# Chunk products of a gated linear recurrence: from 128-token tiles to pairs of 64-token tiles in the matmul array

## The chip, the cores and the metric

The kernel runs on one core of a Trainium2 chip. The metric is the device time of one execution, in microseconds; lower is better. Three executions of the kernel before took 3016.31, 3017.25 and 3018.32 us, median 3017.25 us. The inputs are float32. Matrix products are made by TensorE (PE in the profile) from an SBUF operand that is loaded into the array first (`lhsT`, the weights) and one that is streamed past it (`rhs`, the moving operand), into PSUM. VectorE (DVE), ScalarE (ACT) and GpSimd (POOL) do the rest, and most transfers are issued from SyncE's queue (SP).

## The reference

One decoder layer for 2048 prompt tokens and 32 sample tokens: norm and input projection, then a gated linear recurrence (HGRN2, 4 heads of 128 features) beside a dilated window attention, output projection, a gated feed-forward block with a short convolution, and a gated embedding. The change touches the recurrence of the prompt alone. Cut to that:

```python
def gla_chunked(q, k, v, logf, s0, chunk):
    """S_t = diag(f_t) S_{t-1} + k_t v_t^T, o_t = S_t^T q_t, evaluated chunkwise."""
    ...
    def step(s, xs):
        qc, kc, vc, gc = xs
        b = jnp.cumsum(gc, axis=2)
        o_inter = jnp.einsum('bhtk,bhkv->bhtv', qc * jnp.exp(b), s)
        diff = b[:, :, :, None, :] - b[:, :, None, :, :]
        decay = jnp.exp(jnp.where(causal[:, :, None], diff, -jnp.inf))
        scores = jnp.einsum('bhtk,bhsk,bhtsk->bhts', qc, kc, decay)
        o = o_inter + jnp.einsum('bhts,bhsv->bhtv', scores, vc)
        b_last = b[:, :, -1]
        s = jnp.exp(b_last)[..., None] * s + jnp.einsum(
            'bhsk,bhsv->bhkv', kc * jnp.exp(b_last[:, :, None] - b), vc)
        return s, o
```

with k = 1 - f. The decay between two tokens s < t is a product of the f of the tokens between them, separately for each feature, so `scores` is no plain matrix product.

## The kernel before, in words

The program has four stages that follow each other on PE. First the input projection of prompt tokens 0 to 1023 (block 0, to about 315 us of the profile's span). Then the input projection of the other 1024 prompt tokens and the 32 sample tokens (block 1, `in_phase(1, ...)`, about 315 to 835 us). Then the attention (about 835 to 1235 us), and the rest of the layer (`trunk`). The projections are made with a hi/lo split of both operands, three matmuls for one (lines 142 to 144 and 344 to 346), accumulated over eight k tiles.

The recurrence works in units: `hgrn_unit` does 512 tokens of two heads. There are 8 units (4 stretches of tokens, 2 pairs of heads). It is a generator that yields between its steps; `first(side, n)` advances it by n steps after each step of the main work, with a higher priority in the scheduler. Units 0 to 6 run inside block 1, and unit 7 (`apart=True`, with more yields) runs inside the attention. A scheduler then sets the order on each engine by its own estimates; only in the attention is PE's order that of the code. Every engine works its own list in order.

In a unit, tokens are the columns and the 128 features the partitions. Per head it loads `q`, `f`, `g` (128 x 512, pieces of 2 KB) and `v` (line 446, pieces of 512 bytes), and makes `F` = 1 - f (the keys, line 448) and `E` = q f (line 450). The 512 tokens are four chunks of 128. A chunk's scores (source token s by target token t, tile `at`) are gathered in parts:

- The diagonal s = t: `F` times `q`, one matmul of 128 x 128 per chunk (line 460), then a product with the identity on DVE that also clears the rest of `at` (line 461).
- Three levels, `LEVELS` = 1, 4, 16. A level with width hw handles the pairs of blocks of hw tokens and of 2 hw tokens: it collects the columns of `E` that belong to right-hand blocks in tile `M` (named `hM`), three groups of 64 columns per chunk (two copies on ACT, lines 469 and 474, one product on POOL, line 476). It multiplies `F` of the chunk with these 192 columns (`level_products`, line 484, four matmuls per head and level), grows `E` and `F` by the decays of the level on DVE (`scale`, line 423, and `grow`), and writes the parts of the result that belong to this level into `at` by six masked copies of 128 x 128 (`copy_predicated`, line 496).
- The last level, 64 by 64 tokens of a chunk, has a matmul of its own with 64 columns of weights (line 516) and a copy into the upper right quarter of `at` (line 520).

Then `F` is transposed (529), the state is advanced (541, 545), the output is `at` times `v` plus `E` times the state (552, 553), normed, transposed (574) and written out (576). `E` of the next unit goes into a buffer that is free once line 553 of the unit before has read it.

Matmuls on float32 operands stand in the trace as two records each, with a weight load each: line 484 has 336 matmul records in units 0 to 6, for 168 matmuls. A matmul with 64 columns of weights has the shape 128*64 in the profile, and with `tile_position=(0, 64 * half)` it sits in one half of the array's columns. Line 822 (attention) already does that, with the halves taking turns. Line 338 does it with quarters (128*32).

The quoted code is that of before:

Of the kernel before, what the change touches and what calls it, by code (L numbers as in the profile page):

```python
# [20 lines left out]
D = 1024  # L21
# [26 lines left out]
def hymba_step_kernel(ctx: ExitStack, tc: tile.TileContext, I: dict, O: dict):  # L48
# [386 lines left out]

    def hgrn_unit(u, heads, S, ld, wk, sp, plv, po, pms, msk, apart=False):

        u0 = 512 * u
        st = {}
        for h in heads:  # L440
            t = {}
            for nm, src in (("f", ha_d[1]), ("q", ha_d[0]), ("g", ha_d[2])):
                t[nm] = ld.tile([128, 512], F32, name="h" + nm)
                SP.dma_start(t[nm], src[:, h, u0:u0 + 512])
            t["v"] = ld.tile([128, 4, 128], F32, name="hv")
            SP.dma_start(t["v"], va_d[u0:u0 + 512, 128 * h:128 * h + 128].rearrange("(c s) d -> s c d", s=128))
            t["F"] = wk.tile([128, 512], F32, name="hF")
            G.tensor_scalar(t["F"], t["f"], -1.0, 1.0, op0=ALU.mult, op1=ALU.add)
            t["E"] = wk.tile([128, 512], F32, name="hE")
            G.tensor_mul(t["E"], t["q"], t["f"])  # L450
            t["D"] = t["f"]
            t["at"] = wk.tile([128, 4, 128], F32, name="at", bufs=4)
            st[h] = t
        yield
        for h in heads:
            t = st[h]
            ps = plv([128, 4, 128])
            for c in range(4):
                cs = slice(128 * c, 128 * c + 128)
                PE.matmul(ps[:, c], lhsT=t["F"][:, cs], rhs=t["q"][:, cs], start=True, stop=True)  # L460
            V.tensor_mul(t["at"], ps, ident.rearrange("p (o t) -> p o t", o=1).to_broadcast([128, 4, 128]))
        yield

        def level_operands(t, hw):
            E, D = t["E"], t["D"]
            M = t["M"] = wk.tile([128, 3, 4, 64], F32, name="hM")
            slots = lambda i, n: M[:, i].rearrange("p c (n h) -> p (c n) h", h=n)
            er = pairs(E, hw)[1]
            A.copy(slots(0, hw), er)
# [4 lines left out]
            A.copy(slots(1, 2 * hw), er)  # L474
            d = D.rearrange("p (n four) -> p n four", four=4)[:, :, 1:2]
            G.tensor_mul(slots(2, 2 * hw), er, d.to_broadcast(list(er.shape)))

        def level_products(t):
            pss = t["pss"] = []
            for i in range(2):  # L480
                ps = plv([128, 512])[:, :384].rearrange("p (a c t) -> p a c t", a=3, c=2)
                for c in range(2):
                    cc = 2 * i + c
                    PE.matmul(ps[:, :, c], lhsT=t["F"][:, 128 * cc:128 * cc + 128], rhs=t["M"][:, :, cc],  # L484
                              start=True, stop=True)
                pss.append(ps)

        def level_results(t, li, hw):
# [3 lines left out]
            t["D"] = D4  # L492
            for j in range(2):
                at = t["at"][:, 2 * j:2 * j + 2].rearrange("p c t -> p (c t)")
                for a, n in enumerate((hw, 2 * hw, 2 * hw)):
                    V.copy_predicated(pairs(at, n)[1], msk[:, 3 * li + a].rearrange("p (n h) -> p n h", h=n),
                                      t["pss"][j][:, a].rearrange("p c (n h) -> p (c n) h", h=n))

        for li, hw in enumerate(LEVELS):
            for h in heads:  # L500
                level_operands(st[h], hw)
                if not apart:
                    level_products(st[h])
            for h in heads:
                if apart:
                    yield
                    level_products(st[h])
                    yield
                level_results(st[h], li, hw)
            yield  # L510
        for h in heads:
            t = st[h]
            E, F = t["E"], t["F"]
            ps = plv([128, 4, 128])
            for c in range(4):
# [1056 lines left out]
    def hgrn(lo, hi, *psum, apart=False):  # L1572
        for i in range(lo, hi):
            heads = (0, 1) if i % 2 == 0 else (2, 3)
            yield from hgrn_unit(i // 2, heads, S, ld, wk, sp, *psum, msk, apart)

# [7 lines left out]
    def begin():  # L1584
        mskf = wk.tile([128, 9, 128], F32, name="hM")
        SP.dma_start(mskf, I["lvl_mask"])
        V.tensor_copy(msk, mskf)
        return hgrn(0, 4, *psum)
# [13 lines left out]
    msk = hc.tile([128, 9, 128], U8, name="msk")  # L1602
    side = begin()
    main, rest = None, []
# [60 lines left out]
def _constants():  # L1665
# [19 lines left out]
    c["amask"] = np.where(count == 0, BIG, np.where(count == 2, -np.log(2.0), 0.0)).astype(f)  # L1685
    m = np.zeros((128, 9, 2, 64), f)
    for li, h in enumerate(LEVELS):
        for a, n in enumerate((h, 2 * h, 2 * h)):
# [4 lines left out]
            m[:, 3 * li + a] = part[:, None]  # L1693
    m = m.reshape(128, 9, 128)
    c["lvl_mask"] = m
    j = np.arange(NS)
# [102 lines left out]
```

## Time and profile before

| | us |
|---|---|
| median of three runs (lowest, highest) | 3017.25 (3016.31, 3018.32) |
| profiled execution, time | 3014.84 |
| its span, first to last instruction | 3013.0 |
| granted TensorE clock over the span | 0.988 |
| block 1 with units 0 to 6, 315 to 785 us: span, PE busy, DVE busy, ACT busy, POOL busy | 470, 467.3, 340.7, 134.0, 107.0 |
| attention with unit 7, 840 to 935 us: span, PE busy, DVE busy | 95, 78.3, 74.5 |

The profiled execution is 2.4 us below the median of the runs. Busy time of PE is a union of records that overlap, and their ends are modelled. What a matmul occupies is therefore read from the distance between starts, in a row of the timeline of several equal records: the length of the row, less that of one record, by the number of records less one.

### The profile page before, as it was taken

What the parts mean: (1) busy time and instruction counts of PE and PEld (TensorE: products, weight loads), DVE (VectorE), ACT (ScalarE), POOL (GpSimd) and SP (SyncE); (2) the same over time, 40 slices, a digit from 0 to 9 for tenths busy, and PEclk for the clock granted to TensorE, in tenths of its full rate; (3) what the DMA queues carried; (4) which work ended last, traced back from release to release, by engine and by line L of the source; (5) the groups of instructions that cost most, each with busy time, mean ns of one, the idle gap of its engine ahead of it and who ended that gap; (6) DMA issues with size and microseconds to landing.
All of it is one profiled execution on the core that took longest, in us unless ns stands there. A gap on an engine that the chain in (4) does not pass through costs nothing.

```text
span 3013.0 us, 52001 instructions
## 1 busy us (share of the span) xinstructions
PE 2926.5 (97%) x18639; PEld 2738.0 (91%) x18639; DVE 2191.6 (73%) x4761; ACT 1304.5 (43%) x2824; POOL 667.9 (22%) x780
## 2 busy tenths in 40 slices
PE   8999999999978989999999999999999999999998
PEld 8977789987767667999999999999999999999997
DVE  7666868884466557568988889766769777777777
ACT  5333423231156665334444444544444544444443
POOL 1443222221134553102443431000001000000000
PEclk9999999999989999999999999999999999999999
DMA  5898533342248996766666568677778777778873
GB/s 174 311 337 309 198 103 110 104 134 95 91 115 243 303 246 194 260 225 222 227 209 194 191 198 300 231 250 252 245 231 311 242 245 244 257 248 290 272 274 131
DMA packets 328579, 664.08 MB, mean 220 GB/s; under 512 B 46400, under 2 KB 114112, under 8 KB 326528
## 3 DMA queue, kind: packets, MB, share of 16 engines
q1 hardware_dynamic: 291472, 472.65, 48.4%
q0 software_dynamic: 33264, 121.13, 12.6%
q10 hardware_dynamic: 3584, 66.98, 6.1%
q8 instruction: 147, 2.41, 0.3%
q14 instruction: 112, 0.92, 0.1%
HBM read 513.69 MB, written 213.92 MB: 241 GB/s over the span
## 4 chain that ended last, share of the span: by engine, by line
PE 72%; issue 9%; DVE 7%; DMA 7%; ACT 2%; POOL 2%; SPq 1%; DVEq 0%; POOLq 0%; ACTq 0%
PE mm L142 16%; PE mm L144 16%; PE mm L143 16%; PE mm L346 2%; PE mm L344 2%; PE mm L345 2%; PE lv L484 2%; PE acc L822 2%; PE S L797 1%; PE PT L810 1%; PE S L798 1%; DMA draw<-in_w_down_dram 1%; DMA xr<-in_xT_dram 1%; DVE h L1291 1%; DMA wd_d<-dw 1%
## 5 line engine op out<-in xcount | busy, mean ns | idle before, releaser
L143 PE MATMUL mm<-w 128*128 128x348 f32 (+3 forms) x3636 | 1166.1, 321 | 1.1 <-DVE w L1435 0.7
L142 PE MATMUL mm<-w 128*128 128x348 f32 (+3 forms) x3508 | 1109.7, 323 | 15.2 <-ACT s L1233 5.8
L144 PE MATMUL mm<-w 128*128 128x348 f32 (+3 forms) x3508 | 1117.4, 321 | 1.3 <-DVE w L181 1.3
L143 PEld LDWEIGHTS mm<-w 128*128 128x128 f32 x3636 | 684.3, 188 | 3.8 <-DVE w L1067 1.8
L142 PEld LDWEIGHTS mm<-w 128*128 128x128 f32 x3508 | 656.5, 188 | 23.6 <-ACT s L1233 8.5
L144 PEld LDWEIGHTS mm<-w 128*128 128x128 f32 x3508 | 659.0, 188 | 2.6 <-DVE w L181 1.8
L181 DVE TENSOR_TENSOR w<-raw,w 128x512 fp32r<-128x512 f32 x586 | 421.9, 725 | 170.3 <-ACT w L180 165.3
L180 ACT CAST w<-raw 128x512 fp32r<-128x512 f32 x586 | 360.6, 621 | 402.8 <-PE mm L144 293.1
L1275 POOL DMA_DIRECT2D w<-wd_d x231 | 123.8, 536 | 906.2 <-PE mm L144 800.6
L1291 DVE TENSOR_TENSOR h<-h,mm 128x348 f32<-128x348 f32 (+1 forms) x504 | 248.4, 509 | 45.9 <-PE mm L144 44.4
L803 ACT ACTIVATE P<-P,st 128x256 f32<-128x256 f32 (+3 forms) x256 | 134.1, 526 | 87.5 <-DVE st L802 85.9
L802 DVE CUSTOM_DVE_ANT_0 P<-S,mask 128x256 f32<-128x256 f32 (+3 forms) x256 | 105.0, 449 | 73.1 <-PE S L798 50.1
L1233 ACT COPY s<-mm 128x348 f32<-128x348 f32 (+1 forms) x198 | 87.9, 444 | 158.1 <-PE mm L144 157.8
L345 PE MATMUL mm<-wl,xh 128*128 128x512 f32 x352 | 140.7, 400 | 1.1 <-DVE wl L267 1.1
L344 PE MATMUL mm<-wh,xh 128*128 128x512 f32 x352 | 140.6, 403 | 0.0
L346 PE MATMUL mm<-wh,xl 128*128 128x512 f32 x352 | 140.3, 399 | 0.0
L142 PE MATMUL mm<-xh,wh 128*128 128x384 f32 (+2 forms) x384 | 125.7, 332 | 8.6 <-ACT xh L242 5.1
L143 PE MATMUL mm<-xl,wh 128*128 128x384 f32 (+2 forms) x384 | 126.9, 333 | 0.8 <-DVE xl L243 0.8
L144 PE MATMUL mm<-xh,wl 128*128 128x384 f32 (+2 forms) x384 | 125.5, 330 | 1.5 <-DVE wl L267 1.4
L267 DVE TENSOR_TENSOR wl<-wraw,wh 128x512 fp32r<-128x512 f32 x104 | 86.3, 851 | 34.0 <-POOL wh L148 28.9
L181 DVE TENSOR_TENSOR dw<-draw,dw 128x512 fp32r<-128x512 f32 x77 | 69.4, 909 | 55.8 <-ACT dw L180 55.0
L797 PE MATMUL S<-kH,qS 128*128 128x256 f32 (+3 forms) x256 | 97.7, 396 | 8.2 <-DVE st L802 7.3
(348 smaller groups left out, 5155.0 us busy)
## 6 DMA issues: line engine op xcount, KB each, us to landing
w<-wd_d POOLq DMA_DIRECT2D x231, 512.0 KB, 5.6
wd_d<-dw SPq DMA_DIRECT2D x77, 512.0 KB
out_sk_dram<-in_cache_k_dram ACTq DMA_DIRECT2D x56, 584.0 KB
out_sv_dram<-in_cache_v_dram ACTq DMA_DIRECT2D x56, 584.0 KB
raw<-in_w_gate_dram SPq DMA_DIRECT2D x110, 256.0 KB
raw<-in_w_up_dram SPq DMA_DIRECT2D x110, 256.0 KB
wraw<-in_w_in_dram SPq DMA_DIRECT2D x104, 256.0 KB
raw<-w_gate_d SPq DMA_DIRECT2D x88, 256.0 KB
```

Source lines behind the costliest of these rows:

```text
L142: PE.matmul(ps, lhsT=wh, rhs=xh, start=first, stop=False, skip_group_check=read)
L143: PE.matmul(ps, lhsT=wh, rhs=xl, start=False, stop=False, skip_group_check=read)
L144: PE.matmul(ps, lhsT=wl, rhs=xh, start=False, stop=last, skip_group_check=read)
L180: A.copy(w[:, 0], raw)
L181: V.tensor_sub(w[:, 1], raw, f32(w[:, 0]))
L344: PE.matmul(ps, lhsT=xh[k][:, js], rhs=wh, start=k == 0, stop=False)
L345: PE.matmul(ps, lhsT=xh[k][:, js], rhs=wl, start=False, stop=False)
L346: PE.matmul(ps, lhsT=xl[k][:, js], rhs=wh, start=False, stop=k == NK - 1)
L797: PE.matmul(s[:, w * i:w * i + w], lhsT=bl.q(hh), rhs=bl.k(kH, hh), start=True, stop=False)
L803: A.activation(pe, pe, AF.Exp, bias=mn, scale=-1.0, accum_out=st[:, bl.r, hh, 0:1])
L1275: G.dma_start(t, wd_d[p][n - 1])
L1291: V.tensor_add(o, o, acc[m][:, :H])
```

## The change

The products of the three levels stay within 64 tokens, since the widest pair at level 16 is two blocks of 32. The change computes them by halves of a chunk. For each of the eight blocks of 64 tokens, `F` of the block (64 columns of weights) meets the columns of `M` of the same block only: 3 x 32 in place of 3 x 64. The two blocks of a chunk are put side by side in the array by `tile_position=(0, 64 * half)`, and their results lie in the lower and the upper 64 partitions of one PSUM tile. The scores go to a tile `blk` of 4 x 64 columns in place of `at` with 4 x 128.

`M` is now one tile per head with room for five groups of 32 columns per block. The first two hold `q`, which is loaded straight into them (pieces of 256 bytes), and the first level's matmul takes all five groups: the diagonal is in its result, and the matmul of line 460 with its step (one yield) is gone. In the first level a head's results take two PSUM tiles, in the others one. DVE then multiplies the first two groups by `diag` (four products of 2 x 32 columns per head, new) and makes six masked copies of 64 columns per head at the first level and three of 128 at each of the others, in place of 18 of 128. Before the outputs, `at` is put together: the lower left quarter is cleared on POOL and the two diagonal quarters are copied from `blk` on ACT. `M` has two buffers, so `q` of the next unit can be loaded when the third level's products of this unit have read theirs; the mask's float copy passes through one of the same buffers at the start.

```diff
             t = {}
-            for nm, src in (("f", ha_d[1]), ("q", ha_d[0]), ("g", ha_d[2])):
+            for nm, src in (("f", ha_d[1]), ("g", ha_d[2])):
...
+            M = t["M"] = ld.tile([128, 8, 5, 32], F32, name="hM")
+            q = M[:, :, :2].rearrange("p b two t -> p b (two t)")
+            SP.dma_start(q, ha_d[0][:, h, u0:u0 + 512].rearrange("p (b t) -> p b t", t=64))
...
-            G.tensor_mul(t["E"], t["q"], t["f"])
+            G.tensor_mul(t["E"].rearrange("p (b t) -> p b t", t=64), q, t["f"].rearrange("p (b t) -> p b t", t=64))
...
-            t["at"] = wk.tile([128, 4, 128], F32, name="at", bufs=4)
+            t["blk"] = wk.tile([128, 4, 64], F32, name="blk")
...
-        for h in heads:
-            t = st[h]
-            ps = plv([128, 4, 128])
-            for c in range(4):
-                cs = slice(128 * c, 128 * c + 128)
-                PE.matmul(ps[:, c], lhsT=t["F"][:, cs], rhs=t["q"][:, cs], start=True, stop=True)
-            V.tensor_mul(t["at"], ps, ident.rearrange("p (o t) -> p o t", o=1).to_broadcast([128, 4, 128]))
-        yield
...
-            M = t["M"] = wk.tile([128, 3, 4, 64], F32, name="hM")
...
-        def level_products(t):
-            pss = t["pss"] = []
-            for i in range(2):
-                ps = plv([128, 512])[:, :384].rearrange("p (a c t) -> p a c t", a=3, c=2)
-                for c in range(2):
-                    cc = 2 * i + c
-                    PE.matmul(ps[:, :, c], lhsT=t["F"][:, 128 * cc:128 * cc + 128], rhs=t["M"][:, :, cc],
-                              start=True, stop=True)
-                pss.append(ps)
+        def level_products(t, li):
+            lo, step = (0, 2) if li == 0 else (2, 4)
+            t["pss"] = []
+            for c0 in range(0, 4, step):
+                ps = plv([128, 512])[:, :32 * step * (5 - lo)].rearrange("p (a c t) -> p a c t", a=5 - lo, c=step)
+                for c in range(step):
+                    for half in range(2):
+                        b = 2 * (c0 + c) + half
+                        PE.matmul(ps[64 * half:64 * half + 64, :, c], lhsT=t["F"][:, 64 * b:64 * b + 64],
+                                  rhs=t["M"][:, b, lo:], start=True, stop=True, tile_position=(0, 64 * half))
+                t["pss"].append(ps)
...
-            for j in range(2):
-                at = t["at"][:, 2 * j:2 * j + 2].rearrange("p c t -> p (c t)")
+            step = 4 // len(t["pss"])
+            for j, ps in enumerate(t["pss"]):
+                blk = t["blk"][:, step * j:step * j + step]
+                if li == 0:
+                    for two in range(2):
+                        V.tensor_mul(blk[:, :, 32 * two:32 * two + 32], ps[:, two],
+                                     diag[:, two:two + 1].to_broadcast([128, step, 32]))
                 for a, n in enumerate((hw, 2 * hw, 2 * hw)):
-                    V.copy_predicated(pairs(at, n)[1], msk[:, 3 * li + a].rearrange("p (n h) -> p n h", h=n),
-                                      t["pss"][j][:, a].rearrange("p c (n h) -> p (c n) h", h=n))
+                    V.copy_predicated(pairs(blk.rearrange("p c t -> p (c t)"), n)[1],
+                                      msk[:, 3 * li + a, :32 * step].rearrange("p (n h) -> p n h", h=n),
+                                      ps[:, a + (2 if li == 0 else 0)].rearrange("p c (n h) -> p (c n) h", h=n))
...
+            at = t["at"] = wk.tile([128, 4, 128], F32, name="at", bufs=4)
+            G.memset(at[64:, :, :64], 0.0)
+            for half in range(2):
+                hs = slice(64 * half, 64 * half + 64)
+                A.copy(at[hs, :, hs], t["blk"][hs])
...
     def begin():
-        mskf = wk.tile([128, 9, 128], F32, name="hM")
+        mskf = ld.tile([128, 8, 5, 32], F32, name="hM").rearrange("p b a t -> p (b a t)")[:, :1152]
+        mskf = mskf.rearrange("p (a t) -> p a t", a=9)
         SP.dma_start(mskf, I["lvl_mask"])
+        SP.dma_start(diag, I["diag"])
```

The scheduler places the new matmuls anew. On PE, in unit 1 beside the last token group of block 1's first weight group, the piece of the difference below has line 484 of before (two matmuls of 128 x 192 at a time) and line 481 of the changed kernel, which takes its place (64 columns of weights by 160 or 96; `hF` are the weights, `hM` streams). Lines 344 to 346 are the projection and line 582 is line 574 of before.

```order
 L345 MATMUL mm<-wl,xh_132 128x512
 L346 MATMUL mm<-wh,xl_140 128x512
+L481 MATMUL lv<-hM,hF 64x5x32 x8
+L481 MATMUL lv<-hM,hF 64x3x32 x3
+L582 MATMUL ms<-c_ident,at 128x128 x8
+L481 MATMUL lv<-hM,hF 64x3x32 x5
 L344 MATMUL mm<-wh,xh_133 128x512
-L484 MATMUL lv<-hM,hF 128x3x64 x2
 L345 MATMUL mm<-wl,xh_133 128x512
 L346 MATMUL mm<-wh,xl_141 128x512
```

A head's level now stands mostly as eight matmuls in one place, where before it stood as two and two between projection matmuls. Over the program line 484 stood in 81 places, of two, four or six matmuls, and line 481 stands in 48 (42 in block 1, 6 in the attention), most of them of eight. A visit to matmuls with 64 or 32 columns of weights, from the 128-column ones and back, is made 26 times in block 1 before (line 516 and line 338) and 60 times in the changed kernel. In the attention four of the six places are visits that were not there, and two stand beside line 822's.

On SP, at the change to block 1's second weight group, the loads of `q` into `hM` (line 447) stand between the weight loads (line 263); before they stood behind them as `hq`, next to the loads of `hv`.

```order
-L576 DMA mix_d<-hg 128x512 x2
+L584 DMA mix_d<-hg 128x512 x2
+L385 DMA va_d<-ev 128x512
 L444 DMA hg<-ha_d 128x512 x2
+L263 DMA wraw<-in_w_in_dram 128x512 x4
+L447 DMA hM<-ha_d 128x8x64
+L263 DMA wraw<-in_w_in_dram 128x512
```

What moved is the load of `q` for the next unit: it is issued ahead of the weights of later k tiles, and it waits for the third level's products of the unit that runs.

More of the change, by code (lines that the diff above doesn't have):

```diff
@@ L434, in grow, with hgrn_unit @@
         scale(pairs(F, h)[0], right)
-    def hgrn_unit(u, heads, S, ld, wk, sp, plv, po, pms, msk, apart=False):
+    def hgrn_unit(u, heads, S, ld, wk, sp, plv, po, pms, msk, diag, apart=False):
         u0 = 512 * u
@@ L449, in hgrn_unit @@
             t["E"] = wk.tile([128, 512], F32, name="hE")
[L450 removed]
+            G.tensor_mul(t["E"].rearrange("p (b t) -> p b t", t=64), q, t["f"].rearrange("p (b t) -> p b t", t=64))
             t["D"] = t["f"]
[L452 removed]
+            t["blk"] = wk.tile([128, 4, 64], F32, name="blk")
             st[h] = t
         yield
[L455 to L462 removed]
         def level_operands(t, hw):
[L465 to L467 removed]
+            E, D, M = t["E"], t["D"], t["M"]
+            slots = lambda i, n: M[:, :, 2 + i].rearrange("p b (n h) -> p b n h", h=n)
+            per64 = lambda x: x.rearrange("p (b n) h -> p b n h", b=8)
             er = pairs(E, hw)[1]
[L469 removed]
+            A.copy(slots(0, hw), per64(er))
             t["D2"] = sp.tile([128, 256 // hw], F32, name=f"D{hw}")
@@ L473, in level_operands @@
             er = pairs(E, 2 * hw)[1]
-            A.copy(slots(1, 2 * hw), er)
+            A.copy(slots(1, 2 * hw), per64(er))
             d = D.rearrange("p (n four) -> p n four", four=4)[:, :, 1:2]
-            G.tensor_mul(slots(2, 2 * hw), er, d.to_broadcast(list(er.shape)))
-        def level_products(t):
-            pss = t["pss"] = []
-            for i in range(2):
-                ps = plv([128, 512])[:, :384].rearrange("p (a c t) -> p a c t", a=3, c=2)
-                for c in range(2):
-                    cc = 2 * i + c
-                    PE.matmul(ps[:, :, c], lhsT=t["F"][:, 128 * cc:128 * cc + 128], rhs=t["M"][:, :, cc],
-                              start=True, stop=True)
-                pss.append(ps)
+            G.tensor_mul(slots(2, 2 * hw), per64(er), per64(d.to_broadcast(list(er.shape))))
+        def level_products(t, li):
[9 more added lines that the diff above has]
+                t["pss"].append(ps)
         def level_results(t, li, hw):
@@ L502, in hgrn_unit @@
                 if not apart:
-                    level_products(st[h])
+                    level_products(st[h], li)
             for h in heads:
@@ L506, in hgrn_unit @@
                     yield
-                    level_products(st[h])
+                    level_products(st[h], li)
                     yield
@@ L1574, in hgrn @@
             heads = (0, 1) if i % 2 == 0 else (2, 3)
-            yield from hgrn_unit(i // 2, heads, S, ld, wk, sp, *psum, msk, apart)
+            yield from hgrn_unit(i // 2, heads, S, ld, wk, sp, *psum, msk, diag, apart)
     def first(gen, n):
@@ L1602, in hymba_step_kernel @@
     msk = hc.tile([128, 9, 128], U8, name="msk")
+    diag = hc.tile([128, 2, 32], F32, name="diag")
     side = begin()
@@ L1685, in _constants @@
     c["amask"] = np.where(count == 0, BIG, np.where(count == 2, -np.log(2.0), 0.0)).astype(f)
-    m = np.zeros((128, 9, 2, 64), f)
+    i = np.arange(64)
+    m = np.zeros((64, 9, 4, 32), f)
     for li, h in enumerate(LEVELS):
@@ L1693, in _constants @@
             m[:, 3 * li + a] = part[:, None]
-    m = m.reshape(128, 9, 128)
-    c["lvl_mask"] = m
+    c["lvl_mask"] = np.tile(m.reshape(64, 9, 128), (2, 1, 1))
+    c["diag"] = np.tile(np.eye(64, dtype=f).reshape(64, 2, 32), (2, 1, 1))
     j = np.arange(NS)
```

## The prediction

> **What bounds the kernel now.** I read the page first (busy shares and the chain that ended last), then the busy times by stage, then who PE waited for in the two stages that hold the recurrence.
>
> ```profile
> span 3013.0 us, 52001 instructions
> PE 2926.5 (97%) x18639; PEld 2738.0 (91%) x18639; DVE 2191.6 (73%) x4761; ACT 1304.5 (43%) x2824; POOL 667.9 (22%) x780
> PE 72%; issue 9%; DVE 7%; DMA 7%; ACT 2%; POOL 2%; SPq 1%; DVEq 0%; POOLq 0%; ACTq 0%
> ```
>
> PE is busy for 97% of the span and carries 72% of the chain. That is an average, so here are the stages: block 1 with units 0 to 6, the start of the attention with unit 7, and the rest of the attention (columns: span, then busy us of PE, PEld, DVE, ACT, POOL, granted clock, DMA share, GB/s).
>
> ```profile
> 315.00:785.00 470.00, 467.31 (x2779) 413.28 (x2778) 340.67 (x1003) 133.95 (x360) 107.01 (x131) 1.00 0.36 114
> 840.00:935.00 95.00, 78.28 (x606) 68.96 (x605) 74.45 (x246) 62.10 (x173) 43.63 (x48) 0.89 0.48 128
> 935.00:1235.00 300.00, 280.05 (x2436) 217.73 (x2435) 178.68 (x630) 180.41 (x534) 129.22 (x160) 0.97 0.87 246
> ```
>
> PE's waits, first in block 1 (315 to 785 us), then in the attention with unit 7 (840 to 935 us):
>
> ```profile
> PE lv L484 <- DVE at L461: 1.2, 2, 0.8
> PE lv L484 <- DVE at L496: 0.6, 1, 0.6
> PE mm L142 <- POOL wh L148: 0.3, 1, 0.3
> PE lv L460 <- issue: 0.2, 1, 0.2
> PE mm L144 <- DVE wl L267: 0.2, 1, 0.2
> ...
> PE S L797 <- DVE st L802: 6.3, 2, 4.4
> PE s L574 <- DVE at L567: 5.1, 1, 5.1
> PE s L484 <- DVE at L496: 3.6, 3, 1.6
> ```
>
> In block 1 PE waits 2.5 us out of 470: whatever PE time the recurrence gives back there comes off the end, and relief of DVE, ACT or POOL is worth nothing by itself. In the attention's start PE waits 15 us, all for DVE, so there both engines count.
>
> **What the products cost PE before.** These rows are of block 1, grouped by shape, then a visit of line 484 to the stream of projection matmuls.
>
> ```profile
> L484 PE MATMUL lv<-hM,hF 128*128 128x192 f32 x336 | 67.6, 328 | 2.0 <-DVE at L461 1.2 <-DVE at L496 0.6
> L460 PE MATMUL lv<-hq,hF 128*128 128x128 f32 x112 | 15.5, 275 | 0.2 <-issue 0.2
> L516 PE MATMUL lv<-hE,hF 128*64 128x64 f32 x112 | 9.7, 228 | 0.0
> ...
> 436.15 0.34 PE L142 MATMUL mm<-xh,wh 128*128 128x384 f32 x1
> 436.33 0.81 PE L484 MATMUL lv<-hM,hF 128*128 128x192 f32 x4
> 436.84 0.47 PE L143 MATMUL mm<-xl,wh 128*128 128x384 f32 x1
> 437.15 0.34 PE L144 MATMUL mm<-xh,wl 128*128 128x384 f32 x1
> ```
>
> The four records of 0.81 us, less one of 0.328, are three steps of 0.162 us. Entry and exit are free: 436.33 plus 4 x 0.162 plus one projection step of 0.175 gives 437.15, the start of the second matmul behind. A step of 128 columns is 0.11 us (line 810's row below: 0.60 less 0.27, three steps). Per head (14 heads in block 1): 24 records of line 484 are 3.89 us, 8 of line 460 are 0.90, together 4.79.
>
> **What they cost after.** No row has this matmul. The nearest one is line 822: half-width weights, the two halves in turns.
>
> ```profile
> 951.70 0.60 PE L810 MATMUL PT<-c_ident,P 128*128 128x128 f32 x4
> 952.22 1.09 PE L822 MATMUL acc<-pt,v 128*64 128x128 f32 x16
> ```
>
> Sixteen half-width records of 128 columns take 1.09 less 0.27, so 0.055 us each, where a full-width one takes 0.11: two halves run at once. So I take a pair of records at the price of its columns, 0.162 / 192 = 0.84 ns each: 0.135 us for 160, 0.081 for 96. Per head: 8 pairs of 160 are 1.08 us, 16 of 96 are 1.30, together 2.38. Saved: 4.79 less 2.38 = 2.41 us per head, 33.7 us over 14 heads. If the weight loads of the two halves did not overlap, a pair of 96 could not go below 0.11 us, the full-width step that holds a load of 128 columns; 16 x 0.029 x 14 = 6.5 us is this term's upper bound. Line 822's row can't exclude it, as its pair step is 0.11 anyway.
>
> **What is added on PE: visits.** The array changes shape for a 64-column matmul, and that costs. Line 516 shows it:
>
> ```profile
> 439.61 0.81 PE L484 MATMUL lv<-hM,hF 128*128 128x192 f32 x4
> 440.35 0.68 PE L516 MATMUL lv<-hE,hF 128*64 128x64 f32 x8
> 440.96 0.45 PE L144 MATMUL mm<-xh,wl 128*128 128x384 f32 x1
> 441.24 0.34 PE L142 MATMUL mm<-xh,wh 128*128 128x384 f32 x1
> ```
>
> Line 484's four steps end at 440.26, and line 516 starts at 440.35: 0.09 us lost on entry. Its eight records of 64 columns are worth 8 x 0.054 = 0.43 us, the matmul behind 0.175, yet the second one starts 0.89 us on: 0.28 lost. A visit costs 0.37 us. The order in the section on the change has 60 such visits in block 1 where there were 26: 34 x 0.37 = 12.6 us. PE in block 1: 12.6 less 33.7 = minus 21.1 us.
>
> [...]
>
> **The other engines in block 1.** Rows of before:
>
> ```profile
> L496 DVE COPY_PREDICATED at<-msk,lv 128x128 f32<-128x128 uint8 x252 | 82.0, 342 | 7.3 <-PE lv L484 6.1
> L461 DVE TENSOR_TENSOR at<-lv,c_ident 128x512 f32<-128x512 f32 x14 | 9.3, 683 | 4.3 <-PE o L552 4.3
> L520 ACT COPY at<-lv 64x256 f32<-64x256 f32 x14 | 5.1, 365 | 22.2 <-PE lv L516 17.1 <-DVE at L496 4.4 <-DVE hF L423 0.7
> L476 POOL TENSOR_TENSOR hM<-hE,D 128x256 f32<-128x256 f32 x28 | 20.9, 746 | 104.3 <-DVE hE L423 86.8 <-PE lv L484 10.7 <-DVE rs_t L104 3.8
> L450 POOL TENSOR_TENSOR hE<-hq,hf 128x512 f32<-128x512 f32 x16 | 20.9, 1305 | 40.5 <-PE o L553 40.2 <-DMA hq<-ha_d 0.2
> ```
>
> DVE per head: 18 masked copies at 0.34 and one product at 0.68 go, 6.8 us. Six copies of the same size stay (2.0 us); six copies and four products of 64 columns have no row and lie between half of 0.34 and all of it, so I take 0.25 each, 2.5 us. Saved 2.3 us (1.4 to 3.1). In block 1 PE hides it. ACT gets two copies of line 520's size, 0.73 us per head; POOL a clearing that at most costs line 476's 0.75. Both are busy for under 134 of 470 us and their result is needed only at line 552: nothing, and if a unit's `at` came late, line 552 would stall PE by that 0.7 us, 14 times, 10 us at most.
>
> The load of `q` comes later and in smaller pieces, and the product on POOL (line 450) needs it.
>
> ```profile
> 370.61 0.81 PE L484 MATMUL lv<-hM,hF 128*128 128x192 f32 x4
> ...
> 400.58 1.28 POOL L450 TENSOR_TENSOR hE<-hq,hf 128x512 f32<-128x512 f32 x1 [5.51 <-PE o L553]
> ```
>
> Unit 0's last level is at 370.6 us, and unit 1's line 450 starts at 400.6, held by line 553 of the unit before. That leaves some 30 us for a load of 256 KB, so I cost it at nothing between units. If the cover were gone, every late microsecond would stall PE behind line 481, since PE works in order. Two places remain. In unit 0 the second head's `q` waits for the mask's cast out of the same buffer: plus 1 us (0 to 4; before, the same place cost the 1.8 us that PE waited for lines 461 and 496). And SP can stand at a `q` load with weight loads behind it, which POOL and DVE then turn into `wh` and `wl` for PE: plus 1 us (0 to 8; before, PE waited 0.5 us for these).
>
> **The attention.** Unit 7 has two heads: 4.8 us less on PE, four new visits of 0.37 more, so minus 3.3; DVE minus 4.6. Of the 15 us that PE waits for DVE there part goes, but the softmax's own DVE work stays. Taken: minus 4 (0 to minus 8).
>
> **Sum.** Minus 21.1, plus 1, plus 1, minus 4: minus 23 us, rounded to minus 22, as the steps by columns leave out 1 us of matmuls that the order splits from their partner. The profiled execution took 3014.8 us (span 3013.0), so 2992.8 on its own scale. The median of the runs is 2.4 us above it: 2995. About 0.2%, 6 us, is what a measurement of this kernel can tell from no change.
>
> **The rivals.**
>
> *Loads show.* For it: in line 516's row the narrow matmuls' steps are partly exposed. Then each of the 24 pairs per head adds a load of 64 columns, 0.055 us: 24 x 0.055 x 14 = 18.5 us, and the time is 3014, no change. Against it: line 822's steps are 0.11 us per pair with nothing added. [...] Chance 0.05.
>
> *A wait takes the place.* The first level needs `q`, and PE's list has eight products in one place; with the 4 us, 8 us and 10 us bounds above mostly used, 10 to 15 us come back: 3007. For it: PE runs 21 us ahead of today's schedule, and DVE is 72% busy in block 1 (340.7 of 470). Against it: DVE's load falls more than PE's. Chance 0.18.
>
> *More than forecast.* The attention gives its full 8 us, visits that stand beside each other share an exit, waits stay at nothing: 2986. Chance 0.12.
>
> *Slower: the halves do not run side by side.* Then a head costs 16 x 0.135 + 32 x 0.081 = 4.75 us, as before, and the 34 visits stay: plus 12.6, plus 1.5 in the attention, less some 2 from DVE: 3029. It decides once a pair's step is some 0.065 us above the forecast (21.1 us over 336 pairs), nearly twice. Against it: line 822's same shape and turns. For it: there both halves stream 128 columns, here 96. Chance 0.05.
>
> **How the numbers follow.** Forecast 2995 with chance 0.60. Range 2984 to 3010: low end from minus 8 in the attention and no waits, with shared visits; high end from unshared loads (6.5) and most of the wait bounds. It leaves out the slower case and the no-change one. Faster by over 0.2%: forecast, gains and most of the wait case, 0.86. Within: 0.08, from loads and the worst of the waits. Slower: 0.06.
>
> **What would show it.** Right: line 481's rows have pair steps of 0.08 and 0.135 us, 0.37 us lost per visit, block 1 some 19 to 21 us shorter, PE's waits there still under 6 us. Wrong: single steps of 0.08 us per record (serial halves), about 0.13 us per pair of 96 (loads show), PE waiting on `hM` or on `wh`, or a stage after the attention that grows.

## The result, and the profile after

The changed kernel takes 3008.96 us (median of 7 executions, 3001.74 to 3010.66). The kernel before, beside it on the same chip, takes 3017.56 us (7, 3014.78 to 3020.53). The ratio is 0.9966, 95% interval 0.9955 to 0.9977. A second series gave 3007.90 against 3021.21 us, ratio 0.9951 (0.9936 to 0.9965). So it is faster by 9 to 13 us, where the forecast was 22.

The page of the changed kernel, with the busy time of each engine, answers to the page of before:

```profile
span 3000.0 us, 52488 instructions
PE 2896.2 (97%) x18895; PEld 2695.8 (90%) x18895; DVE 2153.6 (72%) x4713; ACT 1315.5 (44%) x2856; POOL 677.8 (23%) x796
```

PE's busy time fell by 30.3 us (2926.5 less 2896.2) and the span by 13.0: more than half of what PE was relieved of came back as waiting. The next two views cut the span at PE's first score matmul (line 797, now 805) and at its first matmul of the trunk; columns are span, busy us of PE, PEld, DVE, ACT and POOL, granted clock, DMA share, GB/s. Before:

```profile
0.00:837.60 837.60, 817.32 (x4605) 713.90 (x4605) 564.89 (x1431) 253.80 (x574) 223.39 (x245) 1.00 0.53 179
837.60:1212.60 375.00, 338.66 (x2912) 267.31 (x2912) 245.95 (x868) 236.68 (x697) 169.64 (x205) 0.94 0.79 219
1212.60:3013.00 1800.40, 1770.54 (x11124) 1756.83 (x11124) 1380.74 (x2463) 814.00 (x1555) 274.82 (x331) 0.99 0.72 240
```

After:

```profile
0.00:823.00 823.00, 795.47 (x4829) 680.44 (x4829) 530.50 (x1389) 263.77 (x602) 229.01 (x261) 0.99 0.55 182
823.00:1201.90 378.90, 330.88 (x2944) 258.43 (x2944) 238.74 (x862) 237.23 (x701) 170.33 (x205) 0.93 0.77 218
1201.90:3000.00 1798.10, 1769.80 (x11124) 1756.91 (x11124) 1384.36 (x2463) 814.46 (x1555) 278.44 (x331) 0.99 0.72 240
```

Up to the attention PE is busy for 21.9 us less, and the stage is 14.6 us shorter. In the attention PE is busy for 7.8 us less, and the stage is 3.9 us *longer*. The trunk is as it was. This profile is of the fastest of the seven executions. A second one, of an execution of 3015.8 us, has the same shape with a longer attention:

```profile
0.00:827.20 827.20, 798.39 (x4828) 683.13 (x4828) 532.13 (x1389) 263.93 (x602) 228.97 (x261) 0.99 0.55 181
827.20:1212.10 384.90, 335.50 (x2943) 263.16 (x2943) 236.87 (x862) 237.36 (x701) 170.23 (x205) 0.92 0.77 215
```

These are two executions of one program, and they differ by 4.2 us up to the attention and by 6.0 us in it. A difference of that size between two single profiles therefore shows nothing by itself; the ratios of whole series weigh more.

**The new products.** The timeline of PE in the changed kernel, one visit of the first level and one of a later level (line 481 is the new product):

```profile
452.67 0.33 PE L142 MATMUL mm<-xh,wh 128*128 128x384 f32 x1
452.93 1.31 PE L481 MATMUL lv<-hM,hF 128*64 128x160 f32 x16
454.17 0.44 PE L143 MATMUL mm<-xl,wh 128*128 128x384 f32 x1
454.45 0.33 PE L144 MATMUL mm<-xh,wl 128*128 128x384 f32 x1
...
469.70 0.34 PE L142 MATMUL mm<-xh,wh 128*128 128x384 f32 x1
469.97 0.88 PE L481 MATMUL lv<-hM,hF 128*64 128x96 f32 x16
470.78 0.44 PE L143 MATMUL mm<-xl,wh 128*128 128x384 f32 x1
471.06 0.34 PE L144 MATMUL mm<-xh,wl 128*128 128x384 f32 x1
```

The groups of line 481 in block 1 give the length of one record:

```profile
L481 PE MATMUL lv<-hM,hF 128*64 128x96 f32 x448 | 25.0, 252 | 2.5 <-DVE blk L498 2.4
L481 PE MATMUL lv<-hM,hF 128*64 128x160 f32 x224 | 19.0, 307 | 1.7 <-DVE rs_t L104 1.2 <-POOL hM L471 0.5
```

A row of 16 records of 160 columns lasts 1.31 us. Less one record of 0.307 that is 15 steps of 0.067, so 0.134 us for a pair; the row of 96 columns gives (0.88 - 0.252) / 15 x 2 = 0.084. A visit costs 0.35 us: at 160 columns, from 452.67 two projection steps (0.35) and eight pairs (1.07) would put the second matmul behind at 454.09, and it starts at 454.45, so 0.36; at 96 columns 0.34. The visit's exit is there whole: less what is lost on entry (0.09 and 0.10) it costs 0.27 and 0.24 us, where the prediction read 0.28 from the row of line 516, although the pairs cost no more than about the price of their columns (0.134 and 0.084 us against 0.135 and 0.081).

**The new waits.** PE's waits of the changed kernel from 300 us to the attention:

```profile
PE ms L367 <- DVE ev L321: 4.2, 2, 3.9
PE lv L481 <- DVE blk L498: 2.4, 2, 1.2
PE ms L582 <- DVE at L575: 1.9, 1, 1.9
PE lv L481 <- DVE rs_t L104: 1.2, 1, 1.2
```

The first row was there before, with 3.9 us. The second kind was there too: PE waits until DVE has read a PSUM tile, 1.8 us at lines 461 and 496 before, and now 3.1 us (2.4 here and 0.7 at line 524). New are the waits for DVE in the norm of the recurrence's output (line 575) and in a reciprocal square root (line 104), together 3.1 us. Waits for the split weights `wh` and `wl` rose from 0.7 to 2.2 us, and 0.5 us went to `hM` from POOL. In all, PE's idle time from 300 us to the attention rose from 7.8 to 14.3 us.

PE's waits in the attention, before and then in the changed kernel (lines 746 and 743 of before are 754 and 751 of the changed kernel):

```profile
PE S L797 <- DVE st L802: 7.3, 5, 4.4
...
PE PT L746 <- DVE pt L812: 3.9, 2, 3.5
...
PE PT L746 <- POOL w L743: 0.4, 1, 0.4
```

```profile
PE S L805 <- DVE st L810: 8.0, 3, 7.5
...
PE PT L754 <- POOL w L751: 4.0, 1, 4.0
PE PT L754 <- POOL mn L749: 3.7, 1, 3.7
PE PT L818 <- DVE hsat L614: 3.6, 1, 3.6
```

The last three, 11.3 us, are of one kind. A merge of the attention's partial results transposes its coefficients (line 754, where PE waited 4.3 us in all before and waits 10.7 us now), writes them out and loads them back as `cf`; POOL multiplies by them (line 766), DVE adds the results (line 768), and the next merge's weights (lines 748 to 751) stand behind that on POOL. The timeline of one such place in the changed kernel, on PE, on DVE and on POOL; the brackets give the idle time before a row and what ended it:

```profile
1122.47 1.09 PE L818 MATMUL PT<-c_ident,P 128*128 128x128 f32 x4 [3.60 <-DVE hsat L614]
1128.29 0.37 PE L754 MATMUL PT<-c_ident,w 128*16 128x128 f32 x1 [3.68 <-POOL mn L749]
1128.59 0.64 PE L611 MATMUL s<-hsE,hsF 128*32 128x32 f32 x8
```

```profile
1120.88 0.69 DVE L768 TENSOR_TENSOR o<-o,o 128x512 f32<-128x512 f32 x1 [4.65 <-POOL o L766]
...
1121.64 0.68 DVE L820 COPY pt<-PT 128x512 f32<-128x512 f32 x1
1122.24 0.46 DVE L614 COPY_PREDICATED hsat<-msk_s,s 32x32 f32<-32x32 uint8 x4
```

```profile
1118.36 2.48 POOL L766 TENSOR_TENSOR o<-o,cf 128x512 f32<-128x512 f32 x2 [4.59 <-DMA cf<-coef_d]
...
1124.14 2.48 POOL L766 TENSOR_TENSOR o<-o,cf 128x512 f32<-128x512 f32 x2 [3.13 <-DMA cf<-coef_d]
...
1128.06 0.20 POOL L749 TENSOR_TENSOR mn<-wl 128x8 f32<-128x8 f32 x1
```

POOL is held by the coefficients' load (4.59 and 3.13 us), and DVE by POOL's product (4.65 us). Behind that stands the copy of line 820, which has to read PSUM before PE's next transpositions can write there; this is read from the code, as the profile names line 614, right behind the copy on DVE, as what ended the wait. The second wait (3.68 us) is for POOL itself. Between two parts of a merge the side work offers PE only a step of the decode recurrence (line 611, 0.6 us). Why these steps stand there now: the change takes out the step of line 460 with its `yield`, so in the attention, where one step of the side work (unit 7, decode attention, decode recurrence) is taken per turn, and from the 28th turn on in every second turn, everything behind stands one or two turns earlier against the main work.

### The profile page after: what moved, and what is told of

It is laid out like the page before. It is cut to its first block, busy times and chain, and to the rows that moved or that the text cites. A ratio compares the mean times of both kernels' runs of the same rounds, so it can differ in the third digit from the quotient of the medians.

```text
span 3000.0 us, 52488 instructions
## 1 busy us (share of the span) xinstructions
PE 2896.2 (97%) x18895; PEld 2695.8 (90%) x18895; DVE 2153.6 (72%) x4713; ACT 1315.5 (44%) x2856; POOL 677.8 (23%) x796
## 4 chain that ended last, share of the span: by engine, by line
PE 78%; DVE 9%; DMA 8%; issue 2%; ACT 2%; POOL 1%; SPq 1%; DVEq 0%; POOLq 0%; ACTq 0%
PE mm L142 19%; PE mm L143 19%; PE mm L144 19%; PE mm L344 2%; PE mm L346 2%; PE mm L345 2%; PE acc L830 2%; PE S L805 1%; PE PT L818 1%; DVE h L1299 1%; DMA skt<-in_kT_d_dram 1%; DMA xr<-in_xT_dram 1%; DMA wraw<-in_w_in_dram 1%; PE S L806 1%; PE lv L481 1%
```

## The experiments

Each ratio is to the kernel before in the same series on the same chip.

**turn_kept.** The empty turn is put back in unit 7, nothing else.

```diff
         yield
+        if apart:
+            yield
 
         def level_operands(t, hw):
```

> The changed kernel with one empty yield put back in unit 7, where the diagonal's step had been, so that the work beside the attention takes its old turns. Theory (the attention lost time because its side work moved one turn ahead): the attention, 379 us in the changed kernel's profile and 375 before, goes back to 375 or less, and the time falls by 4 to 8 us to about 3001 to 3005. Rival (the attention's difference is chance of the clock, the turn is nothing): within 2 us of the changed kernel, 3007 to 3011.

Measured: 2998.83 us (2994.94 to 3003.05) against 3017.35, ratio 0.9934 (0.9919 to 0.9949). Its attention beside that of the changed kernel:

```profile
823.10:1198.60 375.50, 334.86 (x2943) 260.98 (x2943) 237.54 (x862) 238.21 (x701) 169.12 (x205) 0.93 0.80 220
```

**kept_again.** The same kernel, for a second profile.

> The kernel of turn_kept once more, for a second profile beside two of the changed kernel. Theory: an attention of 374 to 378 us without the waits of PE for POOL's merge (under 2 us in all), and 2996 to 3001. Rival (the first look was a lucky one): an attention of 380 to 386, as the changed kernel's two.

Measured: 3003.34 us (3000.26 to 3008.83) against 3020.21, ratio 0.9945 (0.9928 to 0.9962); an attention of 378.7 us. Both numbers lie above what was expected, so part of the first series' gain was luck. Still, in neither profile does PE wait over 0.9 us for POOL at a merge, and both attentions are at or under the changed kernel's shorter one. Over both series of each, an empty turn makes the changed kernel faster by about 0.2%, 6 us (0.9934 and 0.9945 against 0.9966 and 0.9951).

**before_turn_gone.** The other side: in the kernel before, unit 7's step of line 460 stays, its `yield` goes.

```diff
             V.tensor_mul(t["at"], ps, ident.rearrange("p (o t) -> p o t", o=1).to_broadcast([128, 4, 128]))
-        yield
+        if not apart:
+            yield
```

> The kernel before, with the yield behind the diagonal's step left out in unit 7 alone: the products are all as before, the side work beside the attention moves one turn ahead. Theory (the turn): the attention grows by 3 to 8 us and the time to about 3021 to 3025. Rival (not the turn): 3016 to 3019, as before.

Measured: 3023.65 us (3013.99 to 3029.04) against 3017.35, ratio 1.0018 (1.0005 to 1.0031): the missing turn alone costs the old kernel 5 to 6 us, with the same instructions on PE, DVE, ACT and POOL. At the merges' transposition PE waits 9.8 us, where it waited 4.3 us before:

```profile
842.60:1226.70 384.10, 337.66 (x2911) 267.47 (x2911) 244.06 (x867) 236.96 (x697) 170.82 (x205) 0.93 0.77 216
```

```profile
PE PT L747 <- DVE pt L813: 6.7, 2, 5.5
...
PE PT L747 <- POOL w L744: 3.1, 1, 3.1
```

Up to the attention every engine has the same list in this kernel as in the one before, and that stage took 842.6 us against 837.6 all the same; the attention's 9.1 us more need not all be the turn's.

**turn_two.** Two empty turns in unit 7 in place of one.

> The changed kernel with two empty turns in unit 7 in place of the one that turn_kept has. It tells whether the turn works by how long the recurrence's steps last beside the attention, or by which step stands beside which. Theory (length: each turn later covers more of the attention's waits at its end): 2994 to 2999, as turn_kept or a little under. Rival (place: only the old alignment fits, any shift costs): 3003 to 3010, as the changed kernel.

Measured: 3013.05 us (2996.47 to 3027.52) against 3018.94, ratio 0.9978 (0.9963 to 0.9994). The theory of length fell, and the time lies past the rival's range too. More turns are not better: an attention of 385.4 us with other waits (6.4 us at line 821 for ACT's `pt`, 5.0 at line 676). That it matters which step stands beside which, as the rival has it, fits this, but the loss is larger than it allowed.

**turn_late** and **turn_last.** The empty turn is put in later places of the side work: behind unit 7, or behind the decode attention.

```diff
         yield from hgrn(7, 8, ..., apart=True)
+        yield
         for h in range(4):
```

```diff
+        yield
         with ExitStack() as st:
             yield from hgrn_sample(pools(st)("hsp", 1), pps)
```

> The changed kernel with one empty turn, put behind unit 7 and ahead of the decode attention, in place of the one at unit 7's start. Unit 7's steps then stand one turn early, as in the changed kernel, and all that comes behind them stands as before. Theory (the loss is in the decode steps and in the last merge that they no longer cover): 2997 to 3001, as turn_kept. Rival (the loss is in unit 7's own steps beside the attention): 3006 to 3011, as the changed kernel.

> The changed kernel with one empty turn between the decode attention and the decode recurrence, in place of the one at unit 7's start. Unit 7 and the decode steps stand one turn early, as in the changed kernel; the recurrence's short steps stand against the merges as before. Theory (in the two profiles of the changed kernel PE waits 11.3 and 11.1 us in three places where the recurrence's short steps, or nothing, stand between the parts of a merge that waits for its coefficients' load): those waits go, 2998 to 3002. Rival (the early decode steps and unit 7 cost as much): 3004 to 3010, as turn_late or the changed kernel.

Measured: turn_late 3003.93 us (3000.76 to 3013.14) against 3017.55, ratio 0.9958 (0.9943 to 0.9972); turn_last 3002.88 us (3001.23 to 3005.32) against 3020.21, ratio 0.9948 (0.9935 to 0.9961). Both lie between their two numbers. In turn_last the decode recurrence's steps alone stand a turn later. PE's waits for POOL and for the recurrence at the merges are 3.7 us in place of 11.3, and the attention is 377.9 us, 1 us shorter than the shorter one of the changed kernel:

```profile
PE PT L754 <- POOL w L751: 3.7, 2, 2.9
```

So the turn's place does change the merges' waits. That these waits are what costs the time is not shown: turn_last's interval overlaps those of both series of the changed kernel, and serial_halves below has the same three waits (3.4, 3.2 and 3.1 us) in an attention of 377.3 us.

**turn_mask** and **before_mask.** A second suspicion was the attention's start. The timeline of PE there, before and then after (line 805 of the changed kernel is line 797 of before; line 460 is the removed diagonal):

```profile
839.56 3.72 PE L460 MATMUL s<-hq,hF 128*128 128x128 f32 x16
847.72 0.50 PE L797 MATMUL S<-kH,qS 128*128 128x128 f32 x1 [4.44 <-DVE st L802]
```

```profile
824.70 0.44 PE L806 MATMUL S<-kL,qS 128*128 128x128 f32 x1
832.65 0.50 PE L805 MATMUL S<-kH,qS 128*128 128x128 f32 x1 [7.51 <-DVE st L810]
```

PE waits for DVE, and DVE for the mask's load (9.3 us in the changed kernel). The 3.7 us of line 460 lay in that hole, so taking them out gave nothing there. turn_mask is turn_kept with the mask loaded at the program's start, before_mask is before with the same edit:

```diff
-        mask = wk.tile([128, 768], F32, name="mask", bufs=1)
-        SP.dma_start(mask, I["amask"])
+        mask = amask
...
+    amask = rows.tile([128, 768], F32, name="mask")
+    SP.dma_start(amask, I["amask"])
```

> The changed kernel with the turn of unit 7 kept (as in turn_kept) and with the attention's mask in a tile of its own that is loaded at the program's start. Theory (in the profile after, the matmuls at the attention's start stand 7.5 us behind a DVE that waits 9.3 us for the mask; before, the diagonal's q matmuls of unit 7 lay in that hole, 3.7 us, so taking them out gave nothing there): without the hole the attention is 4 to 7 us shorter than in turn_kept, so 2992 to 2995. Rival (the hole is filled by the clock or by work that would come later anyway: what starts earlier waits later for something else): 2997 to 3000, as turn_kept.

> The kernel before with the mask loaded at the program's start, nothing else. Theory: its hole is smaller, as the diagonal's q matmuls of unit 7 lay in it; PE waits 4.4 us there before. So 2 to 4 us faster than before (3013.5 to 3015.5), less than the mask gives in turn_mask against turn_kept. Rival: the same 4 to 7 us as there, 3010 to 3013, so that the mask has nothing to do with the missed gain. Rival two: no change within 2 us of before.

Measured: turn_mask 3000.30 us (2995.73 to 3003.54) against 3018.94, ratio 0.9937 (0.9926 to 0.9949), as turn_kept; before_mask 3019.89 us against 3018.94, ratio 1.0010 (1.0000 to 1.0021). The theory fell in both; the first came out as its rival, the second as its rival two. The hole closes and others open: turn_mask's attention is 375.8 us long, and among its waits are

```profile
PE s L483 <- DVE blk L500: 6.5, 2, 4.6
...
PE PT L755 <- DVE pt L821: 4.2, 2, 3.8
```

where turn_kept had 2.6 and 0.2 us. That removed work which lay in the hole gave nothing stays true of the place; that the hole itself costs the kernel its length does not.

**old_unit7** and **new_unit7.** The two forms are mixed: units 0 to 6 new with unit 7 as before (its turn too), and the other way round (without the turn). The old form's `M` lies in the load pool's `hM` buffers in both, which before it did not.

```diff
-            yield from hgrn_unit(i // 2, heads, S, ld, wk, sp, *psum, msk, diag, apart)
+            if i in OLD:
+                yield from hgrn_unit_old(i // 2, heads, S, ld, wk, sp, *psum, msk2, apart)
+            else:
+                yield from hgrn_unit(i // 2, heads, S, ld, wk, sp, *psum, msk, diag, apart)
```

> Units 0 to 6 by the changed form, unit 7 by the old one (its mask is loaded beside the new one). Theory (block 1 gains some 15 us, the attention takes part of it back): the attention at 373 to 377 us as before, block 1 14 to 16 us shorter, the time about 3002 to 3004. Rival (block 1 itself gives only some 9 us and the attention nothing): 3007 to 3011.

> The kernel before with unit 7 alone in the new form (halves side by side, the diagonal's q in the first level, one turn less); units 0 to 6 as before. Theory (the attention lost by the change through the missing turn and the uncovered mask, whatever block 1 does): 3 to 7 us slower than before, 3020 to 3024. Rival (the attention's loss was one of how block 1 hands over, or of the run): the form saves its 4 us of PE there, 3013 to 3017.

Measured: old_unit7 3009.16 us (3004.55 to 3011.81) against 3017.35, ratio 0.9969 (0.9955 to 0.9983), no better than the changed kernel. The time lies in the rival's range, but not for the rival's reason: the first stage is 819.5 us, the full gain, and it is the attention that is long:

```profile
819.50:1200.90 381.40, 340.00 (x2911) 266.06 (x2911) 246.06 (x867) 235.75 (x697) 170.01 (x205) 0.94 0.79 215
```

That is 6.4 us more than before, though unit 7 has its old form and its turn, and PE works the same list there as in the kernel before. So the turn is not all that sets the length of this stage. The lists of the other engines differ in places, and single profiles scatter; which of these it is, no run shows.

new_unit7 3028.01 us (3025.94 to 3035.60) against 3018.94, ratio 1.0036 (1.0024 to 1.0048): unit 7's new form without its turn is a loss by itself, 381.0 us of attention against 375.0, and this is larger than forecast. (Its first stage is 843.3 us, 5.7 more than in before's profile. before_mask, whose products are those of before, has 843.3 too, so that the buffers of `M` need not be the reason.)

**unit7_twice** and **twice_again.** turn_kept with each product of unit 7's levels issued twice, to ask whether PE time counts beside the attention.

```diff
-                        PE.matmul(ps[64 * half:64 * half + 64, :, c], ...)
+                        for _ in range(2 if apart else 1):
+                            PE.matmul(ps[64 * half:64 * half + 64, :, c], ...)
```

> The kernel of turn_kept with each product of unit 7's three levels issued twice, the second over the first: 16 pairs of 160 columns at 0.136 us and 32 of 96 at 0.082 more, 4.8 us of PE, about what the change took out of unit 7. Theory (PE time taken out beside the attention gives nothing, as turn_kept's attention is 375.5 us long and that of before 375.0): 2997 to 3002, within 2 us of turn_kept. Rival (PE time counts there, and something else of the change cost as much): 3003 to 3006.

> The kernel of unit7_twice once more, for a second profile: in the first the attention was 3.7 us longer than in turn_kept and the trunk, whose program is the same, 10 us. Theory (the trunk's 10 us are of that one execution, the attention's are what the doubled products cost): an attention of 379 to 384 us and a trunk of 1798 to 1802. Rival (what the attention leaves behind makes the trunk slower each time): a trunk of 1806 to 1812.

Measured: unit7_twice 3010.67 us (3003.45 to 3014.88) against 3017.55, ratio 0.9977 (0.9968 to 0.9986), some 0.4% above turn_kept and past both ranges; twice_again, a single execution, took 3006.08 us. So the theory that the time stays within 2 us of turn_kept fell. The two profiles, attention and trunk of each:

```profile
824.00:1203.20 379.20, 341.57 (x3040) 268.60 (x3040) 240.20 (x862) 238.33 (x701) 168.76 (x205) 0.93 0.80 218
1203.20:3013.10 1809.90, 1775.97 (x11124) 1762.98 (x11124) 1387.60 (x2463) 813.74 (x1555) 274.56 (x331) 0.99 0.71 238
```

```profile
821.30:1200.30 379.00, 344.09 (x3040) 268.95 (x3040) 240.84 (x862) 238.36 (x702) 169.36 (x205) 0.92 0.79 218
1200.30:3004.30 1804.00, 1772.85 (x11124) 1759.95 (x11124) 1382.58 (x2463) 813.01 (x1554) 275.72 (x331) 0.99 0.71 239
```

The attention is 0.3 to 3.7 us longer than turn_kept's 375.5 and 378.7, less than the 5.9 us added (13.2 us busy for these products in unit7_twice, up to 935 us, where turn_kept has 7.3; the expectation's estimate was 4.8) and about what those two differ from each other, 3.2 us, so the profiles do not show that PE time counts in the attention. Most of the 0.4% lies in the trunk, 1804 to 1810 us against 1799.9 and 1799.8, whose program is the same; the second profile's 1804 lies between the two ranges that were expected. Why the trunk is longer is open.

**serial_halves.** The changed kernel with the loop over halves outside the loop over chunks: first all products of one half of the array, then all of the other.

```diff
-                for c in range(step):
-                    for half in range(2):
+                for half in range(2):
+                    for c in range(step):
```

> The changed kernel with the loops over halves and chunks exchanged, so that the same matmuls come in another order: first those of one half of the array, then those of the other. Theory (the gain of the products is the pairing of the halves): no pair runs together, a record of 96 columns takes 0.081 us and one of 160 0.135, and block 1 grows by 33 us, the time to about 3040. Rival (the gain is the smaller number of columns, and the array pairs them in any order): within 5 us of the changed kernel.

Measured: 3005.58 us (3004.72 to 3006.98) against 3017.35, ratio 0.9956 (0.9941 to 0.9972), no slower than the changed kernel, as the rival had it. The theory that the turns of the halves make the pairing fell. The scheduler also placed the matmuls anew, in 55 places of block 1 where it was 42. The rows show why no strict turns were needed: the later level's 16 records, then the groups.

```profile
464.63 1.26 PE L481 MATMUL lv<-hM,hF 128*64 128x96 f32 x16
...
466.11 0.34 PE L142 MATMUL mm<-xh,wh 128*128 128x384 f32 x1
```

```profile
L481 PE MATMUL lv<-hM,hF 128*64 128x96 f32 x448 | 36.5, 253 | 3.0 <-DVE blk L498 2.3 <-DVE rs_t L103 0.8
L481 PE MATMUL lv<-hM,hF 128*64 128x160 f32 x224 | 19.7, 309 | 1.8 <-DVE rs_t L104 1.8
```

In the first level (four records of one half, then four of the other) the group is as short as with turns, 19.7 us against 19.0. In the later levels (eight and eight) it is 36.5 against 25.0: from the row's start to the second matmul behind 1.48 us against 1.09, 0.39 more, where eight pairs taken one after the other would add 0.67 (eight times 0.084, an estimate from the row with turns). So halves that stand four records apart overlap nearly as with turns (0.7 us more over the whole group), and of those that stand eight apart a part still overlaps in this row. The 11.5 us that it adds to this group are not seen in the time: the first stage is 826.8 us against 823.0 and 827.2, as PE's time outside its work there is 22.3 us against 27.5 and 28.8. This is a single series beside a changed kernel whose own two differ by 5 us against before.

**after_again.** The changed kernel once more, since its first profile was of its fastest execution.

> The changed kernel once more, unchanged, for a second profile: the first was of its fastest execution (3001.7 us, 7 under its median). It tells where the other executions lose the rest. Theory (the attention with its missing turn): the same block 1 (first score matmul at 820 to 826 us), an attention of 382 to 388 us, a trunk of 1798 to 1801. Rival (the trunk, by its clock or its weights): an attention of 377 to 380 and a trunk of 1804 to 1810.

Measured: 3007.90 us (3001.64 to 3015.80) against 3021.21, ratio 0.9951; the profile is the one shown above. The attention is 384.9 us, as the theory had it, with the same three waits at the merges (4.3, 3.7 and 3.1 us). First stage and trunk lie 1 us over what was expected. Between the two profiles every stage is longer (4.2, 6.0, 3.8 us) and the granted clock over the span lower, 0.983 against 0.987; equal work scatters by that much here.

## Why the prediction was wrong in its size

The forecast was minus 22 us, and minus 9 (first series) and minus 13 (second) came. Both times lie within the range of 2984 to 3010 and beside the 3007 of the rival *a wait takes the place*. That rival put the whole loss into block 1, where 3 to 5 us of it lie, so that its number fits is luck.

- **The products: right.** Pairs were priced at 0.135 and 0.081 us and measured at 0.134 and 0.084. A visit was priced at 0.37 us and measured at 0.35. The sum for PE was minus 21.1 us, and PE's busy time up to the attention fell by 21.9 (817.3 to 795.5), 21.2 of it behind 300 us. The rivals *loads show* and *halves do not run side by side* are refuted by the same rows: a pair of 96 columns takes 0.084 us, where the first put it at 0.136 (0.081 and a load of 0.055) and the second at 0.162.
- **The waits in block 1: mis-sized.** They were put at plus 2 us. PE's time outside its work in the first stage rose from 20.3 us (837.6 less 817.3) to 27.5, plus 7.2, and from 315 to 785 us it is 8.4 us, where under 6 was to show that the prediction is right. Of its two places, the weights gave 1.5 us where 1 was put, and the load of `q` none. The rest is 1.3 us more for DVE's reads of PSUM tiles and 3.6 us for DVE's lines 575 and 104 and for `hM` from POOL, at places that it put at nothing. Single profiles overstate this somewhat: over the three with the products of before up to the attention (before, before_turn_gone, before_mask: 837.6, 842.6, 843.3 us) and the nine with those of the changed kernel and its mask (821 to 829, mean 824.8), the waits rose by 4.8 us, PE's busy time fell by 21.3, and the first stage is 16 us shorter; forecast were 19.
- **The attention: the failing step.** It was put at minus 4 us (0 to minus 8), from 3.3 us less PE and 4.6 us less DVE. PE's work did fall, by 7.8 and 3.2 us of busy time in the two profiles, and yet the stage took 3.9 and 9.9 us longer. The prediction listed the removed step's instructions and not its `yield`, which in this stage is a place in a hand-written interleaving. turn_kept and before_turn_gone show from both sides that the turn is worth about 0.2%, 6 us. How it acts, by the merges' waits or otherwise, is not shown, and old_unit7 has a long attention with its turn in place.
- **The other half of that step.** With the turn kept, the attention is 375.5 and 378.7 us, against 375.0 before: the forecast's minus 4 isn't there either. Line 460 lay in a hole at the stage's start, and where that hole was closed (turn_mask) others opened. Why the stage gives nothing for the PE and DVE time taken out stays open.

With the turn kept, the change does nearly what was forecast: minus 17 to 19 us. That version, turn_kept, is faster than both kernels (against the changed one by its ratios in separate series, 0.9934 and 0.9945 against 0.9966 and 0.9951, where the intervals of the second series of each overlap), and turn_mask equals it. Open remain the longer trunk of unit7_twice and the long attention of old_unit7.

## What to carry to other kernels

Where code is interleaved by generators, a `yield` is an instruction of the schedule: when a step goes, ask what now stands beside what, and first try the change with the empty step left in. Where closing one wait opens others (turn_mask's attention was 375.8 us, turn_kept's 375.5 and 378.7), a microsecond taken out of one engine may be worth nothing, so cost it at zero until a row shows otherwise. When the bounding engine gets shorter, waits that it did not have come into view (here 7.2 us of PE's time up to the attention): list the waits for the other engines behind it, and not only for the operands of what changed.

## What the runs showed of the hardware

- Matmuls on different column halves of the array overlapped though they did not alternate in PE's list (serial_halves): with four records of one half ahead of four of the other the group of 160 columns cost 19.7 us against 19.0 with turns. With eight ahead of eight part of the overlap was lost (36.5 against 25.0, the group of 96 columns).
- Three visits to 64-column weights cost about the same: 0.36 us with 16 records of 160 columns, 0.34 with 16 of 96, and 0.37 with eight of 64 in the kernel before. In these rows the price did not grow with what the visit held.
- The same instructions in an order that differs by one empty step (before_turn_gone) differ in time by 0.18% (0.05 to 0.31%).
- Equal lists scatter. With the same list on every engine, the stage up to the attention took 837.6 us (before) and 842.6 us (before_turn_gone); two executions of the changed kernel had an attention of 378.9 and 384.9 us, at granted clocks of 0.93 and 0.92.
